# A decoder trunk on one core: retention's gate multiplied in two steps, and new constants in the planner's clock of transfers

## The chip, the core and the metric

The kernel runs on one core of a Trainium2 chip. The metric is the device time of one execution in microseconds (us); the median of three runs is given. A traced execution also gives a span, from the first to the last instruction, which is shorter than the device time.

## The reference

Two decoder layers on 256 rows of width 1024, all in float32. Cut to what matters:

```python
for i in range(DEPTH):                       # 2 layers
    h = rms_norm(x, norm_g[i])
    rq, rk, rv, rz, mq, mk, mv, mz = split(h @ w_in[i])          # eight groups of 512 columns
    r_out = retention(rotary(rq), rotary(rk), rv, ret_norm_g[i]) # 4 heads, GroupNorm per head
    r_out = silu(rz) * r_out                                     # retention's gate
    m_out = silu(mz) * moba(rms_norm(mq), rms_norm(mk), mv, rel_bias)
    x = x + concatenate([r_out, m_out]) @ w_out[i]
    gate = sigmoid(rms_norm(x) @ w_ple_gate[i])
    x = x + gate * rms_norm(p[i] @ w_ple[i], ple_norm_g[i])
```

silu(z) is computed as z * (tanh(z/2) + 1) / 2, with the half folded into a factor elsewhere.

## The kernel before

Every weight matmul is made of three TensorE rows: weights and activations are split into a high part (rounded to the matmul's reduced float32) and a low part (the rest), and `mm3` (L360 to L362) adds high x high, high x low and low x high in PSUM. A tile of weights, 128 x 1024, is loaded by SP into one of eight `wst` buffers (L316), its high part is made by a CAST on ScalarE (L321), its low part by a subtract on VectorE (L323), and twelve TensorE rows then use it. Activations reach the form that TensorE needs through `halves` (ScalarE copies a tile into 16-bit halves, L522), `turned` (SP issues a transposing DMA, L532, and VectorE copies the result out, two L541) and `to_parts` (a factor by L555 where there is one, the high part by ScalarE, L558, the low part by VectorE, L560). `a` is such a pair of parts, and m = 0, 1 are the two halves of 128 rows.

A layer runs the projections in the order MQ, MK, RQ, RK, MZ, MV, RV, RZ, with attention's and retention's own matmuls put between them, then the output projection (its second half of rows first, since MoBA's result is ready earlier), then the embedding `embed`, then the gate projection, whose result (`gated`: tanh L1031, two VectorE steps L1034 and L1036) becomes the next layer's `a`. Four PSUM banks `acc` serve the projections in turn, two to a group; a bank is free when its last reader is done.

The order on each engine is not written by hand. `Flow` plans it while the program is built: each piece of work outside TensorE is a generator that yields `ask(engine, cost, ...)`, and the planner lays it in an order given by its own clocks for the five engines and `dma`, a clock for the transfers. With these clocks it decides when SP issues a load and when it issues a transposing DMA (`can`, `backlog`, `lay`; `mb` is a load's size in MB, 0 marks a transposing DMA). All costs in it are constants in the text, and they set the order alone; what runs waits on semaphores.

Retention's end, before: after the matmuls L834, `ret_norm` computes statistics on VectorE, a power on GpSimd (L574) and the normed output RO on ScalarE (four L913 for each m). Apart from that, when RZ's projection is done, `gate` computes tanh on ScalarE (L755) and G = (tanh + 1) * projection on VectorE (L759), which frees the bank of RZ. `ret_gate` then multiplies RO by G (L932) and hands the product to `halves`, `turned` and `to_parts`, which make rows 0 to 3 of `yT`, read by the first half of the output projection.

Of the kernel before, what the change touches and what calls it, by code (L numbers as in the profile page):

```python
# [10 lines left out]
F32 = mybir.dt.float32  # L11
F32R = mybir.dt.float32r
U16 = mybir.dt.uint16
AF = mybir.ActivationFunctionType
ALU = mybir.AluOpType
AX = mybir.AxisListType

P = 128
# [7 lines left out]
GW = 512  # L26
# [55 lines left out]
class Flow:  # L82
# [4 lines left out]
    def __init__(self, slots):  # L87
        self.clock = {PE: 0.0, ACT: 3.0, DVE: 1.0, POOL: 1.0, SP: 0.7}
        self.dma = 0.0
        self.live = []  # L90
        self.free_at = {k: [0.0] * n for k, n in slots.items()}
        self.lent, self.lending = [], False
        self.loaded, self.after_turn = 0.0, False
        self.end = 0.0

    def begin(self, gen, key, at=None):
# [11 lines left out]
    def can(self, c):  # L108
        eng, cost, take, after, mb = c.want
        r = c.ready if c.on in (None, eng) else c.ready + HOP  # L110
        for w in after:
            if not w.done:
                return None
            r = max(r, w.ready + HOP)
        for s in take:
            if not self.free_at[s]:
                return None
            r = max(r, min(self.free_at[s]))
        if mb is None:
            return r  # L120
        r = max(r, self.dma - self.backlog())
        if mb and callable(c.key) and r < c.key():
            for o in self.live:
                if o.want[0] == SP and o.want[4] == TURN:
                    t = self.can(o)
                    if t is not None and t < r + AHEAD:
                        r = max(r, t + 1.3)
        return r

    def backlog(self):  # L130

        return 9.0 if self.dma < 14 else 1.6 if self.dma < 60 else 0.7

    def pick(self):
        by = {}
# [14 lines left out]
    def lay(self, start, c):  # L150
        eng, cost, take, after, mb = c.want
        for s in take:
            t = min(self.free_at[s])
            self.free_at[s].remove(t)
            self.got = None
            for i, (at, names) in enumerate(self.lent):
                if s == "w" and at == t:
                    self.got = self.lent.pop(i)[1]
                    break
        if eng == POOL and start - self.clock[POOL] > 1.5:  # L160
            cost += 0.9
        self.end = self.clock[eng] = start + cost
        c.ready, c.on = self.end, eng
        if mb is not None:
            rate = 3.3 if self.dma < 11 else 2.5
            if mb and self.after_turn:
                self.dma += 1.0
            self.after_turn = not mb
            self.dma = max(self.dma, start + (1.3 if mb else 1.0)) + (rate * mb if mb else 1.4)
            c.ready = self.dma + (0.9 if mb else 0.65)  # L170
            if mb:
                self.loaded = start
            else:
                c.ready += 0.75 * max(0.0, self.loaded + 2.6 - start)
        c.next()
        if c.done:
            self.live.remove(c)
# [57 lines left out]
def ask(eng, cost, take=(), after=(), mb=None):  # L235
    return eng, cost, take, after, mb
# [3 lines left out]
def tile_hybrid_trunk(ctx: ExitStack, tc: tile.TileContext, first, rest, x, pT, ple_g, rel_bias,  # L240
# [277 lines left out]
    def halves(src, name):  # L518

        yield ask(ACT, 0.95, take=("u16",))  # L520
        u = tok_p.tile([P, 2, GW], U16, name="u16", bufs=U_BUFS)
        nc.scalar.copy(u, src.bitcast(U16).rearrange("p (n t) -> p t n", t=2))  # L522
        if name:
            flow.free(name)
        return u
# [37 lines left out]
    def made(a, m, k0, c):  # L563
        for k in range(k0, k0 + 4):
            a.made[m, k] = c
        return c
# [110 lines left out]
    def layer(l, aT):  # L677
# [3 lines left out]
        def stats(m):  # L681
            return ST_X[l, m, "v"]

        def need_stats(m):
            return (ST_X[l, m],)
# [76 lines left out]

        def after_proj(g, m, ps):
            fn, slack = {MQ: (qk_norm, -3 if l else 2), MK: (qk_norm, -3 if l else 0), RQ: (rope, 4), RK: (rope, 2), MZ: (gate, 4),
                         MV: (value, 1), RV: (value, -4), RZ: (gate, -4)}[g]
            c = flow.begin(fn(g, m, ps), flow.soon(slack))
            {MV: VC, RV: VC, MZ: GC, RZ: GC}.get(g, TC)[g, m] = c
            if g == RZ:
                YC[m, 0] = made(yT, m, 0, flow.begin(ret_gate(m), flow.soon(-5)))

        def project(gs, by_m=False):
            ps = {}
# [151 lines left out]
            flow.lend("T", "T")  # L924
            flow.lend("V", "PS")

        def ret_gate(m):
            while m not in RC:
                yield ask(DVE, 0.0, after=(GC[RZ, m],))
            yield ask(DVE, 0.605, take=("tok",), after=(RC[m], GC[RZ, m]))  # L930
            y = tok_p.tile([P, GW], F32, name="tok")
            nc.vector.tensor_tensor(y, RO[m], G[RZ][:, m], op=ALU.mult)  # L932
            if m:
                flow.free("G")
                flow.free("T")
                flow.lend("T", "G")
            u = yield from halves(y, "tok")
            yield from to_parts(yT, m, 0, u, par[:, Q_RG + l * H:Q_RG + (l + 1) * H])

# [208 lines left out]
```

## Time and profile before

| | |
|---|---|
| median of 3 runs | 306.11 us (305.75 to 306.51) |
| the profiled execution | 305.53 us, span 303.6 us |
| granted TensorE clock | 0.998 |
| busy: TensorE, VectorE, ScalarE, GpSimd | 298.5, 249.8, 208.4, 31.9 us |
| instructions | 4209 |
| read from HBM | 57.42 MB |

The profiled execution lies 0.58 us below the median and 1.93 us above its own span. In rows of the trace the first number is the start in us from the span's start and the second the time in us that the row took; "x2" says that it stands for two instructions, and square brackets give the idle time of the engine before it and what ended it. TensorE rows overlap (a row of 512 columns is listed with 0.39 us), so their pace is read from their starts. SPq rows are the issue of a transfer by SP.

### The profile page before, as it was taken

The page shows a single profiled execution, that of the slowest core. Times are in us where ns is not written, and L with a number is a line of the kernel's source. Part 1 is how long each engine was busy: PE and PEld are TensorE (multiplying, and loading weights), DVE is VectorE, ACT ScalarE, POOL GpSimd, SP SyncE. Part 2 cuts the span into 40 slices and gives each one's busy share as a digit, 9 for nine tenths or more (in the row PEclk, how much of TensorE's full clock was granted, in tenths as well). Part 3 has the DMA queues.
Part 4 walks back from the last instruction along what each step waited for, and adds up shares of the span by engine and source line. Part 5 has one row for each costly group of instructions (what it writes and reads, how often), then busy time and mean ns, then how long its engine had stood idle before and what let it go on. Part 6 is the DMA issues. An engine that isn't in the chain of part 4 may idle for free.

```text
span 303.6 us, 4209 instructions
## 1 busy us (share of the span) xinstructions
PE 298.5 (98%) x1393; PEld 248.3 (82%) x1393; DVE 249.8 (82%) x459; ACT 208.4 (69%) x356; POOL 31.9 (11%) x44
## 2 busy tenths in 40 slices
PE   8999999999999999999999999999999999999994
PEld 4888888888888888888888888888888888888883
DVE  4996897996989897889988789986589689879932
ACT  4976949956746966978567894937473787598411
POOL 6005200000003000130001220000000040001100
PEclk9999999999999999999999999999999999999999
DMA  7998999989699295786697879577966964967011
GB/s 255 400 404 319 293 263 255 193 203 348 242 253 407 85 225 202 164 253 229 150 264 183 304 181 258 109 197 193 353 271 143 350 271 120 310 178 204 22 71 69
DMA packets 61773, 69.76 MB, mean 230 GB/s; under 512 B 46260, under 2 KB 47032, under 8 KB 61624
## 3 DMA queue, kind: packets, MB, share of 16 engines
q1 hardware_dynamic: 61712, 69.50, 75.6%
q8 instruction: 11, 0.18, 0.2%
q14 instruction: 10, 0.08, 0.1%
q0 software_dynamic: 32, 0.01, 0.0%
q10 hardware_dynamic: 8, 0.00, 0.0%
HBM read 57.42 MB, written 1.05 MB: 193 GB/s over the span
## 4 chain that ended last, share of the span: by engine, by line
PE 98%; DVE 0%; ACT 0%; issue 0%
PE acc L362 28%; PE acc L361 28%; PE acc L360 28%; PE acc L456 4%; PE mix L834 4%; PE mix L823 2%; PE mix L275 1%; PE mix L651 1%; PE mix L653 1%; PE mix L652 1%; PE mix L885 1%; PE mix L886 1%; ACT tmp L1031 0%; DVE tmp L1034 0%; DVE x_t L1036 0%
## 5 line engine op out<-in xcount | busy, mean ns | idle before, releaser
L360 PE MATMUL acc<-wh,a 128*128 128x512 f32 (+1 forms) x332 | 128.4, 387 | 0.0
L361 PE MATMUL acc<-wl,a 128*128 128x512 f32 (+1 forms) x332 | 127.5, 384 | 0.0
L362 PE MATMUL acc<-wh,a 128*128 128x512 f32 (+1 forms) x332 | 127.5, 384 | 0.0
L323 DVE TENSOR_TENSOR wl<-wst,wh 128x1024 fp32r<-128x1024 f32 x83 | 100.0, 1222 | 17.2 <-ACT wh L321 16.0
L321 ACT CAST wh<-wst 128x1024 fp32r<-128x1024 f32 x83 | 85.6, 1056 | 34.1 <-DMA wst<-in_w_in 23.7
L362 PEld LDWEIGHTS acc<-wh,a 128*128 128x128 f32 x332 | 62.4, 188 | 12.3
L360 PEld LDWEIGHTS acc<-wh,a 128*128 128x128 f32 x332 | 62.4, 188 | 12.2
L361 PEld LDWEIGHTS acc<-wl,a 128*128 128x128 f32 x332 | 62.4, 188 | 12.2
L522 ACT COPY u<-tok 128x1024 uint16<-128x1024 uint16 x30 | 30.9, 1049 | 8.0 <-DVE tok L852 3.8
L558 ACT CAST a<-tmp 128x512 fp32r<-128x512 f32 x20 | 12.3, 618 | 15.8 <-DVE tmp L541 7.4
L574 POOL TENSOR_TENSOR ro<-rs_t,neghalf 128x4 f32<-128x4 f32 x4 | 6.8, 1688 | 128.8 <-DVE rs_t L572 128.8
L541 DVE COPY tmp<-w 128x512 uint16<-128x512 uint16 x40 | 16.0, 451 | 1.8 <-DMA w<-u 1.8
L522 ACT COPY u<-x_t 128x1024 uint16<-128x1024 uint16 x12 | 12.5, 1045 | 5.0 <-DVE x_t L1036 3.8
L560 DVE TENSOR_TENSOR a<-tmp,a 128x512 fp32r<-128x512 f32 x20 | 13.6, 683 | 2.7 <-ACT a L558 2.7
L1031 ACT ACTIVATE tmp<-acc,hr 128x512 f32<-128x512 f32 (+1 forms) x9 | 5.7, 637 | 13.6 <-PE acc L362 9.3
L541 DVE COPY T<-w 128x512 uint16<-128x512 uint16 x32 | 12.4, 459 | 1.7 <-DMA w<-u 1.7
L715 POOL TENSOR_TENSOR qr<-qms,neghalf 128x4 f32<-128x4 f32 x8 | 9.9, 1314 | 28.8 <-DVE qms L713 28.7
L1034 DVE SCALAR_TENSOR_TENSOR tmp<-tmp,E 128x512 f32<-128x512 f32 (+1 forms) x9 | 5.6, 627 | 7.9 <-ACT tmp L1031 7.9
L834 PEld LDWEIGHTS mix<-V,PS 128*128 128x128 f32 x96 | 11.3, 192 | 0.3
L834 PE MATMUL mix<-V,PS 128*128 128x128 f32 x96 | 11.4, 275 | 0.0
L321 ACT CAST T<-wst 128x1024 fp32r<-128x1024 f32 x8 | 8.4, 1048 | 3.8 <-DMA wst<-in_w_ple 1.9
L574 POOL TENSOR_TENSOR r<-rs_t,neghalf 128x1 f32<-128x1 f32 x4 | 4.0, 992 | 54.8 <-DVE rs_t L572 54.8
(116 smaller groups left out, 367.1 us busy)
## 6 DMA issues: line engine op xcount, KB each, us to landing
wst<-in_w_in SPq DMA_DIRECT2D x60, 512.0 KB, 6.8
wst<-in_w_out SPq DMA_DIRECT2D x16, 512.0 KB, 8.8
wst<-in_w_gate SPq DMA_DIRECT2D x16, 512.0 KB, 4.9
wst<-in_w_ple SPq DMA_DIRECT2D x4, 512.0 KB, 7.5
wst<-in_rest SPq DMA_DIRECT2D x4, 384.0 KB, 6.8
a<-in_rest SPq DMA_DIRECT2D x3, 384.0 KB, 5.0
x_t<-in_x SPq DMA_DIRECT2D x1, 1024.0 KB, 10.4
gb<-in_ple_g SPq DMA_DIRECT2D x2, 512.0 KB, 10.2
```

The lines of the kernel that those rows point to most:

```text
L321: nc.scalar.copy(hi, s)
L323: nc.vector.tensor_tensor(lo, s, hi.bitcast(F32), op=ALU.subtract)
L360: nc.tensor.matmul(ps, ah, wh[:, cols], start=start, stop=False)
L361: nc.tensor.matmul(ps, ah, wl[:, cols], start=False, stop=False)
L362: nc.tensor.matmul(ps, al, wh[:, cols], start=False, stop=stop)
L456: nc.tensor.matmul(ps[m], (a0.lo if which[0] == "lo" else a0.hi)[:, k, m * P:(m + 1) * P], w, start=start and i == 0, stop=stop and i == 2)
L522: nc.scalar.copy(u, src.bitcast(U16).rearrange("p (n t) -> p t n", t=2))
L541: nc.vector.tensor_copy(v, w[:, t].rearrange("p (h b) k -> p h (b k)", h=v.shape[1]))
L558: nc.scalar.copy(h, src)
L560: nc.vector.tensor_tensor(a.lo[:, k0:k0 + 4, m * P:(m + 1) * P], src, h.bitcast(F32), op=ALU.subtract)
L574: nc.gpsimd.tensor_tensor(dst, t[:, :n], neghalf[:, :n], op=ALU.pow)
L834: nc.tensor.matmul(ps[:, h * DH:(h + 1) * DH], lhs(h, m, b), v[:, b, h * DH:(h + 1) * DH], start=b == 0, stop=b == m)
```

## The change

1. For RZ, `gate` is no longer used. A new `ret_tanh` computes tanh on ScalarE (L930); `ret_gate` first multiplies RO by RZ's projection, straight from PSUM (L940), and then computes (tanh + 1) * that product in place (L945). So RZ's bank is free only after L945, and no G is stored for RZ. MZ keeps `gate`.
2. The planner's clock of transfers has new constants and a new form: loads and transposing DMAs run from the time that SP issued them (`issued`), a load follows a transposing DMA with 1.2 us more and a transposing DMA costs 0.9 us of the clock, and the backlog to which it lets loads run ahead is 9.9, 2.5 and 1.6 us where it was 9.0, 1.6 and 0.7. This alters the order on all engines, in both layers. The number and kind of the instructions that compute or move data stays as it was.

```diff
--- before.py
+++ after.py
@@ -90,7 +90,7 @@
         self.live = []
         self.free_at = {k: [0.0] * n for k, n in slots.items()}
         self.lent, self.lending = [], False
-        self.loaded, self.after_turn = 0.0, False
+        self.issued, self.turning = 0.0, False
         self.end = 0.0
 
     def begin(self, gen, key, at=None):
@@ -118,6 +118,7 @@
             r = max(r, min(self.free_at[s]))
         if mb is None:
             return r
+        c.issue = r
         r = max(r, self.dma - self.backlog())
         if mb and callable(c.key) and r < c.key():
             for o in self.live:
@@ -129,7 +130,7 @@
 
     def backlog(self):
 
-        return 9.0 if self.dma < 14 else 1.6 if self.dma < 60 else 0.7
+        return 9.9 if self.dma < 14.9 else 2.5 if self.dma < 60.9 else 1.6
 
     def pick(self):
         by = {}
@@ -162,16 +163,15 @@
         self.end = self.clock[eng] = start + cost
         c.ready, c.on = self.end, eng
         if mb is not None:
-            rate = 3.3 if self.dma < 11 else 2.5
-            if mb and self.after_turn:
-                self.dma += 1.0
-            self.after_turn = not mb
-            self.dma = max(self.dma, start + (1.3 if mb else 1.0)) + (rate * mb if mb else 1.4)
-            c.ready = self.dma + (0.9 if mb else 0.65)
+            at = max(self.issued, c.issue) if self.dma > 14.9 else start
+            self.issued = at + cost
             if mb:
-                self.loaded = start
+                rate = 3.3 if self.dma < 11.9 else 2.55
+                self.dma = max(at + 2.27 + rate * mb, self.dma + rate * mb + 1.2 * self.turning)
             else:
-                c.ready += 0.75 * max(0.0, self.loaded + 2.6 - start)
+                self.dma = max(at + 3.05, self.dma + 0.9)
+            self.turning = not mb
+            c.ready = self.dma
         c.next()
         if c.done:
             self.live.remove(c)
@@ -762,11 +762,11 @@
 
         def after_proj(g, m, ps):
             fn, slack = {MQ: (qk_norm, -3 if l else 2), MK: (qk_norm, -3 if l else 0), RQ: (rope, 4), RK: (rope, 2), MZ: (gate, 4),
-                         MV: (value, 1), RV: (value, -4), RZ: (gate, -4)}[g]
+                         MV: (value, 1), RV: (value, -4), RZ: (ret_gate, -5)}[g]
             c = flow.begin(fn(g, m, ps), flow.soon(slack))
             {MV: VC, RV: VC, MZ: GC, RZ: GC}.get(g, TC)[g, m] = c
             if g == RZ:
-                YC[m, 0] = made(yT, m, 0, flow.begin(ret_gate(m), flow.soon(-5)))
+                YC[m, 0] = made(yT, m, 0, c)
 
         def project(gs, by_m=False):
             ps = {}
@@ -924,16 +924,27 @@
             flow.lend("T", "T")
             flow.lend("V", "PS")
 
-        def ret_gate(m):
+        def ret_tanh(m, ps, mark):
+            yield ask(ACT, 0.59, take=("tmp",), after=need_stats(m))
+            mark.tile = tmp_p.tile([P, GW], F32, name="tmp")
+            nc.scalar.activation(mark.tile, ps, AF.Tanh, scale=stats(m)[1])
+            flow.reach(mark)
+
+        def ret_gate(g, m, ps):
+            th = Mark()
+            flow.begin(ret_tanh(m, ps, th), flow.soon(-5))
             while m not in RC:
-                yield ask(DVE, 0.0, after=(GC[RZ, m],))
-            yield ask(DVE, 0.605, take=("tok",), after=(RC[m], GC[RZ, m]))
+                yield ask(DVE, 0.0)
+            yield ask(DVE, 0.605, take=("tok",), after=(RC[m],))
             y = tok_p.tile([P, GW], F32, name="tok")
-            nc.vector.tensor_tensor(y, RO[m], G[RZ][:, m], op=ALU.mult)
+            nc.vector.tensor_tensor(y, RO[m], ps, op=ALU.mult)
             if m:
-                flow.free("G")
                 flow.free("T")
                 flow.lend("T", "G")
+            yield ask(DVE, 0.605, after=(th,))
+            nc.vector.scalar_tensor_tensor(y, th.tile, 1.0, y, op0=ALU.add, op1=ALU.mult)
+            flow.free("acc")
+            flow.free("tmp")
             u = yield from halves(y, "tok")
             yield from to_parts(yT, m, 0, u, par[:, Q_RG + l * H:Q_RG + (l + 1) * H])
 
```

Where this moves instructions, three places follow: word for word the rows of each engine's order, "x2" for two instructions. Lines of the changed text behind the edit are 11 higher.

In the second layer, VectorE from retention's gate to the first L560 that makes rows 0 to 3 of `yT` (`tok` is the product, L323 are subtracts for weights that come later). Before:

```order
L759 SCALAR_TENSOR_TENSOR G<-tmp,acc 128x512
L932 TENSOR_TENSOR tok<-T,G 128x512
L323 TENSOR_TENSOR wl<-wst,wh 128x1024 x2
L759 SCALAR_TENSOR_TENSOR G<-tmp,acc 128x512
L932 TENSOR_TENSOR tok<-T,G 128x512
L323 TENSOR_TENSOR wl<-wst,wh 128x1024 x2
L541 COPY tmp<-w_2648 128x512 x2
L555 TENSOR_TENSOR tmp<-tmp,par 128x512
L323 TENSOR_TENSOR G<-wst,T 128x1024
L560 TENSOR_TENSOR a<-tmp,a 128x4x128
```

Now, with L940 and L945 for L759 and L932:

```order
L940 TENSOR_TENSOR tok<-T,acc 128x512
L945 SCALAR_TENSOR_TENSOR tok<-tmp,tok 128x512
L323 TENSOR_TENSOR wl<-wst,wh 128x1024
L940 TENSOR_TENSOR tok<-T,acc 128x512
L945 SCALAR_TENSOR_TENSOR tok<-tmp,tok 128x512
L323 TENSOR_TENSOR wl<-wst,wh 128x1024
L541 COPY tmp<-w_2658 128x512 x2
L555 TENSOR_TENSOR tmp<-tmp,par 128x512
L323 TENSOR_TENSOR G<-wst,T 128x1024
L323 TENSOR_TENSOR wl<-wst,wh 128x1024
L560 TENSOR_TENSOR a<-tmp,a 128x4x128
```

From the first product to the L560 there are four subtracts where there were five, and two of them stand behind the copies L541 where there was one.

Between the layers, VectorE from behind the sum of the first `gated` tile to the first L560 that makes the second layer's input (`x_t` is the residual; L1045 and L1047 are L1034 and L1036 of before). Before:

```order
L323 TENSOR_TENSOR wl<-wst,wh 128x1024
L323 TENSOR_TENSOR G<-wst,T 128x1024
L323 TENSOR_TENSOR wl<-wst,wh 128x1024 x2
L1034 SCALAR_TENSOR_TENSOR tmp<-tmp,E 128x512
L1036 TENSOR_TENSOR x_t<-x_t,tmp 128x512
L323 TENSOR_TENSOR T<-wst,T 128x1024
L541 COPY tmp<-w_1556 128x512 x2
L555 TENSOR_TENSOR tmp<-tmp,par 128x512
L1034 SCALAR_TENSOR_TENSOR tmp<-tmp,E 128x512
L1036 TENSOR_TENSOR x_t<-x_t,tmp 128x512
L323 TENSOR_TENSOR PS<-wst,V 128x1024
L560 TENSOR_TENSOR a<-tmp,a 128x4x128
```

Now:

```order
L323 TENSOR_TENSOR G<-wst,T 128x1024
L323 TENSOR_TENSOR wl<-wst,wh 128x1024 x3
L1045 SCALAR_TENSOR_TENSOR tmp<-tmp,E 128x512
L541 COPY tmp<-w_1561 128x512 x2
L555 TENSOR_TENSOR tmp<-tmp,par 128x512
L1047 TENSOR_TENSOR x_t<-x_t,tmp 128x512
L323 TENSOR_TENSOR T<-wst,T 128x1024
L560 TENSOR_TENSOR a<-tmp,a 128x4x128
```

One L1034, one L1036 and one subtract that stood between that sum and its L560 now stand behind the L560.

In the second layer, SP from the last transposing DMA of the attention's probabilities to those of MoBA's result (`pf` and `gb` are the embedding's input and gain). Before:

```order
L532 DMA_TRANSPOSE w_2138<-u_2123 128x8x128
L316 DMA wst<-in_w_in 128x1024 x3
L532 DMA_TRANSPOSE w_2202<-u_2191 128x8x128
L532 DMA_TRANSPOSE w_2213<-u_2200 128x8x128
L316 DMA wst<-in_w_in 128x1024 x7
L293 DMA pf<-in_pT 128x512
L316 DMA wst<-in_w_in 128x1024
L293 DMA gb<-in_ple_g 128x1024
L532 DMA_TRANSPOSE w_2398<-u_2385 128x8x128
L532 DMA_TRANSPOSE w_2420<-u_2414 128x8x128
L316 DMA wst<-in_w_in 128x1024
L316 DMA wst<-in_w_out 128x1024 x8
```

Now:

```order
L532 DMA_TRANSPOSE w_2149<-u_2134 128x8x128
L316 DMA wst<-in_w_in 128x1024 x3
L532 DMA_TRANSPOSE w_2223<-u_2215 128x8x128
L532 DMA_TRANSPOSE w_2235<-u_2221 128x8x128
L316 DMA wst<-in_w_in 128x1024
L293 DMA pf<-in_pT 128x512
L316 DMA wst<-in_w_in 128x1024
L293 DMA gb<-in_ple_g 128x1024
L316 DMA wst<-in_w_in 128x1024
L316 DMA wst<-in_w_out 128x1024 x7
L532 DMA_TRANSPOSE w_2419<-u_2405 128x8x128
L532 DMA_TRANSPOSE w_2442<-u_2433 128x8x128
```

Nine loads of `w_in` stood behind the pair of transposing DMAs in the middle, now three: six have moved ahead of this piece, and seven loads of the output weights now stand ahead of MoBA's pair, where one load of `w_in` and all eight stood behind it.

## The prediction

> **What bounds the kernel.** I read the page first, then who waits for whom on TensorE, then TensorE's rows in order of time, and last the rows of the other engines ahead of the places where TensorE is served latest.
>
> ```profile
> span 303.6 us, 4209 instructions
> PE 298.5 (98%) x1393; PEld 248.3 (82%) x1393; DVE 249.8 (82%) x459; ACT 208.4 (69%) x356; POOL 31.9 (11%) x44
> ...
> PE 98%; DVE 0%; ACT 0%; issue 0%
> ```
>
> TensorE is busy in 298.5 of 303.6 us, and the chain that ended last is TensorE in 98%. That busy time could still hide waits, since its rows overlap. The view of who waited has only this for TensorE:
>
> ```profile
> PE mix L275 <- PEq L1137: 0.8, 1, 0.8
> ```
>
> So I take the starts. First the normal pace, then the two places where the pace breaks, then the end:
>
> ```profile
> 217.15 0.40 PE L360 MATMUL acc<-wh,a 128*128 128x512 f32 x1
> 217.39 0.39 PE L361 MATMUL acc<-wl,a 128*128 128x512 f32 x1
> ...
> 220.79 0.39 PE L361 MATMUL acc<-wl,a 128*128 128x512 f32 x1
> ```
>
> ```profile
> 4.63 1.68 PE L456 MATMUL acc<-wh,a 128*128 128x512 f32 x4
> 6.15 0.62 PE L456 MATMUL acc<-wl,a 128*128 128x512 f32 x2
> ...
> 261.00 0.50 PE L362 MATMUL acc<-V,a 128*128 128x512 f32 x1
> 261.33 0.40 PE L360 MATMUL acc<-V,a 128*128 128x512 f32 x1
> ```
>
> ```profile
> 298.94 0.28 PE L362 MATMUL acc<-wh,a 128*128 128x256 f32 x1
> ```
>
> From 217.15 to 220.79 there are 16 steps, 0.2275 us each: a row of 512 columns starts as soon as the one before is streamed. Four rows take 1.52 us from 4.63 to 6.15, where 4 x 0.2275 = 0.91 were due: 0.61 lost while the first blocks arrive. At 261.00 a step takes 0.33: 0.10 lost. All other steps, taken through the whole trace, are at pace, to some 0.1 us in sum. So TensorE loses about 0.7 us to waits in the whole execution, and of the 4.7 us from the last matmul's start at 298.94 to the end at 303.6 the change alters nothing: the same tanh, two VectorE steps and transfer stand there in both orders.
>
> That is the main reading. The profiled execution took 305.53; 0.3% of the median (306.11) is 0.92 us, about what a measurement of this kernel can tell from no change. Removing every wait of TensorE would bring 0.7. The question is therefore whether the new order makes TensorE wait where it did not.
>
> **The change part by part.**
>
> *The operations themselves.* For RZ in two layers and two halves, four L759 and four L932 become four L940 and four L945; tanh stays.
>
> ```profile
> L759 DVE SCALAR_TENSOR_TENSOR G<-tmp,acc 128x512 f32<-128x512 f32 x8 | 5.4, 688 | 2.3 <-ACT tmp L755 2.3
> L932 DVE TENSOR_TENSOR tok<-T,G 128x512 f32<-128x512 f32 x4 | 2.8, 692 | 0.1
> ```
>
> L759 reads PSUM (`acc`) and takes 688 ns, L932 reads SBUF alone and takes 692: where an operand lies makes no difference here, so the new pair costs 1.38 us, as the old one. Cost 0 on VectorE. What can be gained is latency: L940 needs no tanh.
>
> *Retention's gate in the second layer, the place with the 0.10.* The matmul at 261.00 reads the low part that L560 makes.
>
> ```profile
> 250.65 0.69 DVE L932 TENSOR_TENSOR tok<-T,G 128x512 f32<-128x512 f32 x1
> 251.26 2.36 DVE L323 TENSOR_TENSOR wl<-wst,wh 128x1024 fp32r<-128x1024 f32 x2
> 253.53 0.68 DVE L759 SCALAR_TENSOR_TENSOR G<-tmp,acc 128x512 f32<-128x512 f32 x1
> ...
> 257.13 0.79 DVE L541 COPY tmp<-w 128x512 uint16<-128x512 uint16 x2
> ...
> 260.26 0.68 DVE L560 TENSOR_TENSOR a<-tmp,a 128x512 fp32r<-128x512 f32 x1
> ```
>
> ```profile
> 249.20 0.70 ACT L755 ACTIVATE tmp<-acc,hr 128x512 f32<-128x512 f32 x1
> 249.77 2.02 ACT L321 CAST wh<-wst 128x1024 fp32r<-128x1024 f32 x2
> ```
>
> ```profile
> 252.75 1.24 SPq L532 DMA_TRANSPOSE w<-u  x1
> ```
>
> ```profile
> DMA to landing us min/median/max: 3.0/3.1/4.8
> ```
>
> The last row is for all 42 transposing DMAs. Before, the product was ready at 250.65 + 0.69 = 251.34 and L560 ended at 260.94, 9.60 later, with five subtracts of 1.18 between (2.36 for two). Now one cast (2.02 / 2 = 1.01) stands ahead of tanh on ScalarE that stood behind it; the tanh may start up to 1.01 later, and the product, which then needs one VectorE step behind tanh and not two, is ready 0.69 sooner behind it: between 0.69 earlier and 0.3 later. I take 251.3, between these ends; at 251.6 the cover below is 0.2 and not 0.5. With one subtract less, VectorE would reach the end of L560 at 260.94 - 1.18 = 259.8. The other limit is the transposing DMA: if SP issues it at 252.75 as before, it lands at 252.75 + 3.1 = 255.85, and L541, L555 (as long as L932), now two subtracts, and L560 follow: 0.79 + 0.69 + 2.36 + 0.68 = 4.52, to 260.4. TensorE wants it by 260.9 (261.00 less the 0.10). I take 260.4: the wait of 0.10 goes, cover 0.5. With the longest landing, 4.8, it is 262.1 and the wait 1.2 in place of 0.10: a loss of 1.1. What speaks for a long landing is that SP now issues four gate loads ahead of this DMA; against it, those need a free buffer each and will be issued as the subtracts before 251 release them, some in time to be through.
>
> At this place a page speaks against the change. The Trainium skill, "DMA: Bandwidth & Descriptors", section "Two DMAs through the same engine are not ordered", says that descriptors within one queue of one engine start in order. By that rule a transposing DMA behind loads pays for them, and the sum would be the 1.1 us loss just given, or more with several loads; by the median row it is 0.10 gained. The trace agrees as far as 4.8 against 3.0, no further.
>
> *The bank.* RZ's second bank was freed by L759 at 253.53 + 0.68 = 254.21. It is next written, by the second half of the output projection, here:
>
> ```profile
> 255.79 0.39 PE L360 MATMUL acc<-wh,a 128*128 128x512 f32 x1
> ```
>
> Cover 1.58. Now L945 frees it: 251.34, a subtract, L940, L945, so 251.34 + 1.18 + 0.69 + 0.69 = 253.9. Behind it wait this bank's matmul and with it all of TensorE. Cost 0, cover 1.9; in the first layer the same order stands with more room.
>
> *Between the layers.* VectorE makes the second layer's first input:
>
> ```profile
> 140.01 0.69 DVE L1036 TENSOR_TENSOR x_t<-x_t,tmp 128x512 f32<-128x512 f32 x1
> ...
> 151.53 0.69 DVE L560 TENSOR_TENSOR a<-tmp,a 128x512 fp32r<-128x512 f32 x1
> ```
>
> ```profile
> 152.36 0.41 PE L362 MATMUL acc<-T,a 128*128 128x512 f32 x1
> ```
>
> L560 ends at 152.22, 0.14 before the matmul that reads it. An L1034 (of the form of L759, so 0.69), an L1036 and a subtract now stand behind it: 0.69 + 0.69 + 1.18 = 2.56 us sooner, if the transposing DMA is there. TensorE did not wait, so the gain is 0; the cover grows to about 2.7, and even a landing 1.7 late leaves 1.0.
>
> *Weights of MV and RV in the second layer.*
>
> ```profile
> 190.44 10.19 SPq L532 DMA_TRANSPOSE w<-u  x5
> 200.68 1.53 SPq L316 DMA_DIRECT2D wst<-in_w_in  x3
> 207.15 2.62 SPq L532 DMA_TRANSPOSE w<-u  x2
> 209.82 4.24 SPq L316 DMA_DIRECT2D wst<-in_w_in  x7
> ```
>
> ```profile
> 205.12 1.05 ACT L321 CAST wh<-wst 128x1024 fp32r<-128x1024 f32 x1 [4.80 <-DMA wst<-in_w_in]
> ```
>
> ```profile
> 215.93 1.23 DVE L323 TENSOR_TENSOR wl<-wst,wh 128x1024 fp32r<-128x1024 f32 x1 [1.98 <-ACT wh L321]
> ```
>
> SP's loads wait for the queue's turn behind the transposing DMAs, ScalarE then idles 4.80 for a load, and a subtract ends at 217.16, only 0.23 before L361 at 217.39 reads it. Six loads have moved ahead of this stretch. They gain at least one place each, 4.24 / 7 = 0.6 us, and at most the 10.19 us of the five transposing DMAs, unless no buffer is free, when they gain nothing. I take the low end, 0.6: cover 0.8, time 0. The loads moved ahead also push transposing DMAs, by up to 1.7 (4.8 less 3.1) each; MoBA's pair, which now stands behind seven loads, is wanted only when the output projection starts, after all of RZ: 0.
>
> *Sum.* 303.6 - 0.10 + 0 = 303.5 of span, 305.4 of device time for an execution like the profiled one, which lies 0.58 under the median: 306.0.
>
> **The rivals.**
>
> *Transposing DMAs come late behind the loads* (slower). Place and price as above: behind the four gate loads, TensorE waits from a landing of 3.6 on (cover 0.5), it counts as slower from 4.6, and at 4.8 it costs 1.1: 306.11 + 1.1 = 307.2. For it: 4.8 occurs. Against: the median is 3.1.
>
> *TensorE waits for RZ's bank* (slower). It decides once L945 ends after 255.79. For it: the bank now hangs on the normed output too, which passes GpSimd and ScalarE. Against: a cover of 1.9. A slip of 3 costs 1.1: 307.2.
>
> *A low part comes late at one of the many other moved subtracts* (slower): covers of 0.14 and 0.23 show how near the old order ran to waiting; one subtract out of place costs up to 1.18: 307.3.
>
> *The waits go* (faster): all 0.7 would give 305.4. Against: 0.61 of it stands at the start, where the first loads are ordered as before.
>
> *TensorE waits so long that it slows down.* The trace shows a slow pace only at the start:
>
> ```profile
> 0.76 4.00 PE mix L275 x9
> ```
>
> Nine rows of 512 columns take 0.44 us each, nearly twice 0.2275, for 4.0 us, which is 1.95 lost. A wait of 3 us followed by as long a stretch at that pace would cost 5: 311. No wait in this trace is over 0.61.
>
> The Trainium skill, "TensorE: Matmul & The Clock Gate", section "What's actually happening", has TensorE's clock halved after an idle window of about 3.4 us; no wait in this trace is long enough to show it, and that figure is the page's.
>
> **How the numbers follow.** No measurable change: 0.81, 306.0, its own range 305.5 to 306.6 from the spread of the three runs. Late transposing DMAs 0.06, bank 0.03, another late part 0.05, long wait 0.01: slower by over 0.3%, 0.15 in all. Faster by over 0.3%: 0.04, the 0.7 plus the spread. The range goes from 305.2 to 307.4, over the three slower cases at 307.2 and 307.3.
>
> **What would show it.** Right: TensorE's steps stay 0.2275 at 261, 152 and 217, tanh (L930) no longer ahead of both products, L560 earlier than 260.9 by about 0.5. Wrong: a step longer than 0.3 behind the gate loads, at the output projection's second half or at a weight's first use; or a larger gain, if the end of the program got shorter, which I do not see.

## The result, and the profile after

The change made the kernel slower: 307.92 us median of 7 runs (307.13 to 309.46) against 306.04 of before (305.36 to 306.51). The means stand at a ratio of 1.0071, with a 95% interval of 1.0046 to 1.0095; the loss is under 2% and clear of the noise. The profiled execution took 308.94, the second longest of the seven, so it shows about 1 us more of waiting than a middle one. Its totals:

```profile
span 306.7 us, 4243 instructions
PE 299.5 (98%) x1393; PEld 247.6 (81%) x1393; DVE 249.5 (81%) x459; ACT 206.7 (67%) x356; POOL 30.7 (10%) x44
...
PE 49%; DVE 20%; DMA 15%; ACT 7%; issue 6%; SPq 1%; DVEq 0%; ACTq 0%
```

Each engine works about as long as before. What changed is the chain: TensorE held 98% of it, now 49%, and half of it passes through VectorE, the DMAs and ScalarE. The view of who waited has three names for TensorE, besides the first blocks' loads, that were not there:

```profile
PE acc L362 <- DVE a L560: 1.0, 1, 1.0
PE acc L360 <- DVE tok L718: 0.5, 1, 0.5
PE mix L834 <- ACT V L749: 0.5, 1, 0.5
```

TensorE's rows in order of time show where they stand (the time in brackets is the idle time and what ended it):

```profile
27.38 0.39 PE L362 MATMUL acc<-wh,a 128*128 128x512 f32 x1
28.25 0.50 PE L360 MATMUL acc<-wh,a 128*128 128x512 f32 x1 [0.48 <-DVE tok L718]
```

```profile
92.60 0.39 PE L362 MATMUL acc<-wh,a 128*128 128x512 f32 x1
93.46 0.38 PE L834 MATMUL mix<-V,PS 128*128 128x128 f32 x1 [0.47 <-ACT V L749]
```

```profile
159.80 0.40 PE L361 MATMUL acc<-wl,a 128*128 128x512 f32 x1
161.15 0.50 PE L362 MATMUL acc<-wh,a 128*128 128x512 f32 x1 [0.95 <-DVE a L560]
```

Taken as steps against the pace of 0.2275, with the rows just behind that come in a little slow, these three cost 0.76, 1.14 (0.63 and 0.10 here, 0.31 and 0.10 at the next V) and 1.23; a fourth at 140.4 costs 0.26 (its matmul at 140.82 follows an L560 that ends at 140.77). Together they cost 3.39. Before lost none of it. Against that the start lost 0.12 less, the 0.10 at 261 is gone, and the end behind the last matmul's start was 0.25 shorter: 2.9 of the 3.1 by which the span grew, the rest being rows a few ns off pace.

All four waits lie in layer 1 or between the layers. Behind all of them stands a late VectorE, and behind all but the one at 27.4 it had idled at its copy L541 until a transposing DMA landed. The view of one line, L541, has for before and after:

```profile
  DMA w<-u: 4.3, 4
```

```profile
  DMA w<-u: 17.1, 16
```

VectorE idles 17.1 us there in place of 4.3. The largest piece is at 122, ahead of the wait at 159.8. SP's rows and VectorE's:

```profile
117.89 3.16 SPq L316 DMA_DIRECT2D wst<-in_w_in  x3
122.41 8.79 SPq L532 DMA_TRANSPOSE w<-u  x3
```

```profile
120.62 1.45 DVE L998 TENSOR_TENSOR x_t<-acc,x_t 128x512 f32<-128x512 f32 x2
127.49 0.79 DVE L541 COPY tmp<-w 128x512 uint16<-128x512 uint16 x2 [5.42 <-DMA w<-u]
```

Three loads stand right ahead of the transposing DMA of 122.41; it lands at 127.47, 5.06 after its issue, and VectorE, whose next step in order is the copy of its result, does nothing for 5.42. Before, the same DMA was issued at 119.82 with no load under way and landed after 3.09, and VectorE idled 0.59 at the copy:

```profile
119.82 2.96 SPq L532 DMA_TRANSPOSE w<-u  x2
```

In a table of one stretch, 122 to 136 us, whose columns are TensorE, its weight loads, VectorE, ScalarE and GpSimd, first before and then after:

```profile
122.00:136.00 14.00, 14.00 (x63) 11.62 (x62) 11.71 (x30) 11.76 (x24) 3.66 (x4) 1.00 0.78 199
```

```profile
122.00:136.00 14.00, 14.00 (x64) 11.58 (x63) 7.63 (x17) 10.59 (x20) 1.48 (x1) 1.00 0.74 173
```

VectorE does 7.63 us of work where it did 11.71. TensorE stands 1.9 us further on in the old trace at that time; in the stretch that matches, 120.1 to 134.1, VectorE did 10.20. A further transposing DMA, issued at 129.96, lands 4.86 later and costs VectorE another 0.91. It has nothing to spare afterwards (28.66 of the 29 us from 136 to 165), so the lateness reaches the L560 of 160.41 that TensorE then waits for. At 92.6 it goes another way round:

```profile
88.50 0.46 DVE L541 COPY tmp<-w 128x512 uint16<-128x512 uint16 x1 [1.53 <-DMA w<-u]
```

```profile
90.38 0.62 ACT L558 CAST a<-tmp 128x512 fp32r<-128x512 f32 x1 [4.26 <-DVE tmp L541]
...
92.20 0.62 ACT L558 CAST a<-tmp 128x512 fp32r<-128x512 f32 x1 [0.24 <-DVE tmp L541]
92.72 0.68 ACT L749 ACTIVATE V<-acc,rstd 128x512 f32<-128x512 f32 x1
```

This is MoBA's transposing pair of layer 1. Its first DMA is issued at 84.25 behind four loads of the output weights, two of them still under way, and lands 4.22 later:

```profile
72.64 4.63 SPq L316 DMA_DIRECT2D wst<-in_w_out  x4
84.25 3.13 SPq L532 DMA_TRANSPOSE w<-u  x2
```

TensorE does not need its result yet. But VectorE's copies wait for it, ScalarE's casts L558 wait for VectorE, and the V that TensorE does need stands behind the second cast on ScalarE. Before, the pair was issued at 81.61, ahead of these loads, its first DMA landed after 3.04, and V waited for TensorE:

```profile
87.32 0.62 ACT L558 CAST a<-tmp 128x512 fp32r<-128x512 f32 x1 [3.21 <-DVE tmp L541]
88.95 0.69 ACT L749 ACTIVATE V<-acc,rstd 128x512 f32<-128x512 f32 x1 [1.01 <-PE acc L362]
```

So the DMA lands 3.82 later than before, and only 1.18 of that is a longer landing. The other 2.64 is a later issue: the product L852 that it carries starts at 82.02 where it started at 79.38. One subtract and L674, which stood behind the product before, now stand ahead of it, and VectorE's subtracts on the way wait 2.67 us for weights, where they waited 2.46.

The wait at 27.4 is of a third kind. VectorE idles 0.91 ahead of a subtract whose load landed late, and the L718 that frees TensorE's bank stands behind that subtract. SP issued that load at 13.15, behind the load of a table (`tb`) that stood behind it before, when it went out at 11.62; ScalarE's cast of it starts at 25.28 in place of 22.62. VectorE's rows:

```profile
26.37 1.23 DVE L323 TENSOR_TENSOR wl<-wst,wh 128x1024 fp32r<-128x1024 f32 x1 [0.91 <-ACT wh L321]
27.51 0.68 DVE L718 TENSOR_TENSOR tok<-acc,qr 128x512 f32<-128x512 f32 x1
```

### The profile page after: what moved, and what is told of

Read it like the earlier page. It is cut to its first block, busy times and chain, and to the rows that moved or that the text cites. A ratio compares the mean times of both kernels' runs of the same rounds, so it can differ in the third digit from the quotient of the medians.

```text
span 306.7 us, 4243 instructions
## 1 busy us (share of the span) xinstructions
PE 299.5 (98%) x1393; PEld 247.6 (81%) x1393; DVE 249.5 (81%) x459; ACT 206.7 (67%) x356; POOL 30.7 (10%) x44
## 3 DMA queue, kind: packets, MB, share of 16 engines
HBM read 57.42 MB, written 1.05 MB: 191 GB/s over the span
## 4 chain that ended last, share of the span: by engine, by line
PE 49%; DVE 20%; DMA 15%; ACT 7%; issue 6%; SPq 1%; DVEq 0%; ACTq 0%
PE acc L362 15%; PE acc L360 15%; PE acc L361 15%; DMA w<-u 7%; DMA wst<-in_w_in 6%; DVE wl L323 5%; ACT wh L321 2%; DVE tmp L541 2%; DMA a<-in_rest 2%; PE mix L834 2%; DVE a L560 1%; ACT u L522 1%; DVE tmp L1045 1%; DVE E L641 1%; ACT T L913 1%
## 5 line engine op out<-in xcount | busy, mean ns | idle before, releaser
L360 PE MATMUL acc<-wh,a 128*128 128x512 f32 (+1 forms) x326 | 126.6, 388 | 0.5 <-DVE tok L718 0.5
L362 PE MATMUL acc<-wh,a 128*128 128x512 f32 (+1 forms) x326 | 125.7, 386 | 1.0 <-DVE a L560 1.0
L361 PE MATMUL acc<-wl,a 128*128 128x512 f32 (+1 forms) x326 | 125.6, 385 | 0.0
L323 DVE TENSOR_TENSOR wl<-wst,wh 128x1024 fp32r<-128x1024 f32 x82 | 99.0, 1219 | 11.9 <-ACT wh L321 11.5
L321 ACT CAST wh<-wst 128x1024 fp32r<-128x1024 f32 x82 | 84.4, 1052 | 18.5 <-DMA wst<-in_w_in 12.3
L362 PEld LDWEIGHTS acc<-wh,a 128*128 128x128 f32 x326 | 61.2, 188 | 13.8 <-DVE a L560 1.4
L360 PEld LDWEIGHTS acc<-wh,a 128*128 128x128 f32 x326 | 61.3, 188 | 13.1 <-DVE tok L718 0.9
L361 PEld LDWEIGHTS acc<-wl,a 128*128 128x128 f32 x326 | 61.3, 188 | 11.9
L522 ACT COPY u<-tok 128x1024 uint16<-128x1024 uint16 x30 | 30.9, 1046 | 17.1 <-DVE tok L740 7.4
L541 DVE COPY tmp<-w 128x512 uint16<-128x512 uint16 x40 | 16.4, 455 | 13.6 <-DMA w<-u 13.6
L558 ACT CAST a<-tmp 128x512 fp32r<-128x512 f32 x20 | 12.4, 621 | 21.1 <-DVE tmp L541 12.4
L574 POOL TENSOR_TENSOR ro<-rs_t,neghalf 128x4 f32<-128x4 f32 x4 | 7.6, 1912 | 129.1 <-DVE rs_t L572 129.1
L522 ACT COPY u<-x_t 128x1024 uint16<-128x1024 uint16 x12 | 12.5, 1043 | 8.8 <-DVE x_t L998 6.1
L541 DVE COPY T<-w 128x512 uint16<-128x512 uint16 x32 | 12.6, 456 | 2.5 <-DMA w<-u 2.4
L560 DVE TENSOR_TENSOR a<-tmp,a 128x512 fp32r<-128x512 f32 x20 | 13.6, 682 | 0.0
L1045 DVE SCALAR_TENSOR_TENSOR tmp<-tmp,E 128x512 f32<-128x512 f32 (+1 forms) x9 | 5.6, 628 | 8.2 <-ACT tmp L1042 8.2
L362 PE MATMUL acc<-T,a 128*128 128x512 f32 (+1 forms) x30 | 11.4, 379 | 0.0
L360 PE MATMUL acc<-T,a 128*128 128x512 f32 (+1 forms) x30 | 11.3, 375 | 0.0
```

The costliest lines, as they stand in the source:

```text
L321: nc.scalar.copy(hi, s)
L323: nc.vector.tensor_tensor(lo, s, hi.bitcast(F32), op=ALU.subtract)
L360: nc.tensor.matmul(ps, ah, wh[:, cols], start=start, stop=False)
L361: nc.tensor.matmul(ps, ah, wl[:, cols], start=False, stop=False)
L362: nc.tensor.matmul(ps, al, wh[:, cols], start=False, stop=stop)
L541: nc.vector.tensor_copy(v, w[:, t].rearrange("p (h b) k -> p h (b k)", h=v.shape[1]))
```

## The experiments

Ratios are to the kernel before on the same chip, with 95% intervals. "Late" counts the transposing DMAs in a trace that landed more than 3.5 us after their issue (of 36 to 40 whose landing was recorded): 6 before, 14 after. "Idle" is VectorE's idle time in us ahead of its copies of their results: 4.3 before, 17.1 after. Both are counted in one traced execution of each kernel, which lies up to 1.35 us off that kernel's median. The letters stand for theories; each is stated in the expectation that first uses it.

**Which half of the change.** First the gate alone, with the old clock of transfers.

> The gate's new steps with the order's old clock of transfers. Theory A (the refitted clock lets loads go so early that transposing DMAs land behind them, and VectorE runs late): no part of the loss without it, 305.4 to 306.5 us, ratio to before 0.998 to 1.002, transposing DMAs that land after more than 3.5 us about 6, as before (after: 14). Theory B (splitting the gate moves steps and banks so that TensorE waits): the whole loss, 307.5 to 308.5, ratio about 1.006. Theory C (any other order costs about as much, since the old constants were chosen for the old order): 306.8 to 308, with waits at other places than after's 27.4, 92.6 and 159.8.

e1 took 305.79, ratio 0.9987 (0.9970 to 1.0005), with 9 late and an idle time of 3.8. There is no loss. The only new wait of TensorE in its trace is 0.61 for a subtract at 217.5, where the prediction had read a cover of 0.23. Theory B falls. Then the clock alone, with the gate's code as before.

> The order's new clock of transfers with the gate as it was. Theory A: the whole loss, 307.5 to 308.5 us, ratio 1.005 to 1.009, and over ten transposing DMAs that land after more than 3.5 us. Theory B: none of it, 305.7 to 306.4. Theory C: 306.8 to 308, the same as with the gate alone.

e2 took 307.26, ratio 1.0037 (1.0015 to 1.0058), with 11 late, an idle time of 11.5, and the wait at the same V as above:

```profile
PE mix L834 <- ACT V L749: 1.3, 1, 1.3
```

The loss comes with the clock. It is smaller than expected, though its interval overlaps that of the whole change. Whether the other half needs both parts or is a matter of which order came out, these two runs can't tell.

**The lead of the loads.** The changed kernel with the old lead, and the old kernel with the new:

```
-        return 9.9 if self.dma < 14.9 else 2.5 if self.dma < 60.9 else 1.6
+        return 9.0 if self.dma < 14 else 1.6 if self.dma < 60 else 0.7
```

> The changed kernel with the old lead of loads (9.0, 1.6, 0.7 and the old two limits in place of 9.9, 2.5, 1.6): a load is ordered 0.9 us nearer to its turn. If it is the loads ahead of transposing DMAs that cost (A), fewer land late and most of the loss goes: 306.0 to 307.0 us, ratio 1.000 to 1.003, late ones under ten. If the lead doesn't matter (B, C): 307.5 to 308.5.

> The kernel before with only the new lead (9.9, 2.5, 1.6 with the new limits): in the old clock, which counts a load's delivery apart, this lets each load be ordered 0.9 us further ahead. A: more transposing DMAs land behind loads, over ten late ones, 306.8 to 308 us, ratio 1.002 to 1.006. B: nothing, 305.7 to 306.4.

e3: 307.35, ratio 1.0039 (1.0019 to 1.0059); late 7, idle 11.8. Fewer land late, as theory A said, but half of the loss stays. The traced execution of e3 took 306.45, the shortest of twelve, and its trace shows TensorE waiting only 0.41 behind the first blocks, at a V; it can't show where the middle one loses. e4: 305.46, ratio 0.9992 (0.9974 to 1.0009), and here theory A breaks:

```profile
DMA to landing us min/median/max: 3.0/3.4/6.2
```

15 transposing DMAs are late, one by more than any in the changed kernel, and nothing is lost: VectorE idles 6.3. This suggests that a late transposing DMA costs only where the order puts its copy at the head of VectorE's line too early. The old clock added up to 1.64 us to its landing behind a fresh load (0.75 x (2.6 - 0.42), since a load holds SP's clock for 0.42), so that other work could stand ahead of the copy.

**Four edits of the clock.** In the changed kernel the old surcharge put back (e5, `c.ready += 0.75 * max(0.0, self.loaded + 2.6 - at)` behind a load); in the old kernel the same line taken out (e6); in the changed kernel `AHEAD = 4.0` for 1.6 (e7), and `at = start` for the line that dates a DMA's issue (e8).

> The changed kernel, whose clock again adds to the landing of a transposing DMA what the old one did behind a load (0.75 us for each us by which the load stands less than 2.6 ahead). Theory D (the new clock forecasts transposing DMAs behind loads 0.5 us too early in the mean, VectorE's order is made for that forecast, and VectorE then idles): the idle time of VectorE before L541 falls from 17.1 us to under 8, and most of the loss goes, 305.8 to 306.8 us, ratio 0.999 to 1.003. Theory C (any other order costs, chance decides): 306.8 to 308. Theory E (it is the loads' issue and landing times in the new clock that are wrong, not the transposing DMAs): no change from 307.9 beyond 0.5.

> The kernel before, whose clock no longer adds anything to a transposing DMA's landing behind a load; nothing else changed. Theory D: part of the loss appears, 306.5 to 307.5 us, ratio 1.002 to 1.005, VectorE's idle time before L541 8 to 14 us in place of 4.4. Theory E: no change, 305.7 to 306.4, idle under 7. Theory C: 306.8 to 308.

> The changed kernel with AHEAD at 4.0 in place of 1.6: a load that is not urgent is ordered behind a transposing DMA that is to be issued within 4.0 us. If loads right ahead of the transposing DMAs are the cause, whatever the forecast, late ones fall from 14 to under 8 and the time to 306.0 to 307.0; by D also, since the forecast is then true. By C 306.8 to 308. It may cost at weights that come later: then waits of TensorE on L323 or L321 show, and up to 309.

> The changed kernel with its new clock, but a DMA's issue is again taken where the order puts it, not where it could stand if SP never held it. Theory E: most of the loss goes, 306.0 to 306.8. Theory D: it stays, 307.2 to 308.3, VectorE idle before L541 over 11 us. C: 306.8 to 308.

e5: 306.51, 1.0022 (1.0009 to 1.0035). Two thirds of the loss are gone, as D expected, but the idle time is 12.5 and not under 8. e6: 306.42, 1.0021 (1.0005 to 1.0037); the time came out near what D expected, but the idle time, 6.0, did not, and the one long wait, 0.8 at 219.7, is for a subtract at a weight's first use and not for anything behind a copy. e7: 306.12, 1.0010 (0.9995 to 1.0025): holding loads back behind a coming transposing DMA removes nearly all of the loss, though 11 are still late. e8: 310.94, 1.0158 (1.0129 to 1.0186), outside what any theory gave. Loads now come too late for the weights:

```profile
PE acc L361 <- DVE wl L323: 3.3, 4, 1.5
```

In e8 the waits at 92.6 and 159.8 are gone and VectorE idles only 5.0 at its copies, yet the late weights cost more than the whole change did. So e8 does not decide on theory E: without the new dating of issues one loss goes and a larger one comes. It does show that idle time alone is no measure of the loss: it counts only where somebody on TensorE's path stands behind it.

**The price of a transposing DMA alone.** e9 is the changed kernel with the old price (queue 1.4, landing 0.25 later, surcharge); e10 the old kernel with the new price, `self.dma = max(start + 2.15, self.dma + 0.9)` and no surcharge; e12 is e10's edit on e4; e11 is e4's lead with the new gate.

> The changed kernel and its new clock, in which a transposing DMA alone is again priced as before: it keeps the queue for 1.4 in place of 0.9, lands 0.25 later behind others, and later still behind a fresh load. Theory D (the loss comes from forecasting transposing DMAs too early): the loss goes, 305.6 to 306.7 us, ratio 0.999 to 1.002. Theory F (it is the pace of the loads, 1.28 us for each half megabyte where the old clock held them to 1.85): it stays, 307.3 to 308.3. Theory C (chance): anything from 306 to 308.

> The kernel before with one thing of the new clock: a transposing DMA keeps the queue for 0.9 and lands with its turn, with nothing added behind a load. Loads are priced as before. D: most of the loss appears, 306.8 to 308 us, ratio 1.003 to 1.007, VectorE idle before L541 over 8 us (4.3 before). F: no change, 305.7 to 306.4.

> The new gate with the old clock and the longer lead, the two that did not lose alone (0.9987 and 0.9992). If they add, 305.0 to 305.7 us, ratio 0.996 to 0.999; by theory C (each order has its own waits) 305.4 to 307.

> The old clock with the longer lead, under which 15 transposing DMAs landed late (up to 6.2 us) at no loss, and now with the new price of a transposing DMA. D: as many are late and the order does not expect it, so the loss is as large as after's or larger, 307.3 to 309 us, VectorE idle before L541 over 12 us (6.3 without). F: 305.4 to 306.4, since the loads are priced as in the run without loss.

e9: 307.57, 1.0052 (1.0034 to 1.0070). e10: 305.65, 0.9992 (0.9980 to 1.0004), with an idle time of 9.5. Both speak against theory D as I had put it: the price alone neither makes the loss in the old order nor takes it from the new one. In e9's trace the waits at 92.6 and 159.8 are gone, but VectorE still idles 4.72 at the copy of the place at 122, is busy for 14.68 of the next 15.10 us, and TensorE waits at 140.4 (lines are 4 higher in this kernel):

```profile
PE acc L366 <- DVE her L641: 1.1, 1, 1.1
```

e11: 305.99, 1.0004 (0.9990 to 1.0017); the two that lost nothing alone do not add to a gain, and no version here beats the kernel before by a measurable amount. e12: 311.60, 1.0180 (1.0162 to 1.0199), late 17, idle 18.2 (lines are 1 lower in this kernel):

```profile
PE acc L360 <- DVE wl L322: 1.4, 2, 1.2
PE mix L833 <- ACT V L748: 1.2, 1, 1.2
```

That is more than theory D had expected. Both paths, by VectorE's subtracts and by ScalarE's V, are in its trace. VectorE idles 2.52 at a copy at 54.9 and is then busy without a break until the subtract for which TensorE waits 1.19 at 62.3; it idles 3.63 at a copy at 91.1, ScalarE's cast 6.37 behind it, and V is late again. With the lead of e4 the new price costs 6 us; without it, nothing. In the old clock both must come together: loads close enough ahead to delay the transposing DMAs, and an order made as if they did not. Theory F is not needed for a loss, since e12's loads are priced as e4's; but e9 came out where F said, so the new pace of the loads may still be a second cause. Theory C in its plain form, that any other order costs, falls with e1, e4, e7, e10 and e11, five other orders at no measurable loss.

**The same order with half the bytes.** Every run so far changed the order itself. The last four keep each engine's order and take bytes off the queue. In e13 34.62 MB are read where 57.42 were, and the casts and subtracts, which then read one half twice, take as long as before (1.04 and 1.20 us on average):

```
-            nc.sync.dma_start(s, self.src[:, 2 * c:2 * c + 2])
+            n = 1 if len(cut) in range(9, 999) else 2
+            cut.append(0)
+            nc.sync.dma_start(s[:, :n], self.src[:, 2 * c:2 * c + n])
+            if n == 1:
+                s = s[:, :1].to_broadcast([P, 2, GW])
```

> The changed kernel with every engine's order as it is, but each weight load from the tenth on brings only half of its bytes (the first of two blocks, which cast and subtract then read twice): part of the weights is left out. Theory G (the order is sound, its transfers come later than it was made for): with the queue relieved nearly all waits go, except the one at 27.4, whose load is not halved: 305.6 to 306.6 us, and within 0.8 of the order before with the same halved loads. Theory H (steps stand in a wrong sequence on the engines, whatever the transfers do): 307 to 308, over 1.0 above it.

> The control: the order before with its weight loads halved in the same way from the eleventh on (part of the weights is left out). TensorE hardly waited for transfers there, so by every theory 305.2 to 306.2 us, ratio 0.997 to 1.001.

> The changed kernel's order with only the 14 loads issued between 98 and 137 us halved (part of the weights is left out). If the stall of 1.2 at 159.8 comes from the transposing DMA at 122.4 that lands 5.06 later behind three loads, and the one at 130.0 behind it: it lands within 3.6, VectorE's idle time there falls by over 3 us, the stall shrinks to under 0.3, time 306.4 to 307.2. If the stall comes from the sequence of steps on VectorE: it stays, 307.5 to 308.3.

> The changed kernel's order with only the 20 loads issued between 38 and 77 us halved (part of the weights is left out). If ScalarE's V comes late at 92.6 because the transposing DMA at 84.25 lands 4.2 later behind loads: it lands within 3.3, the waits of TensorE at 92.6 and 94.6 (0.63 and 0.31) go, time 306.6 to 307.4. If it comes from the sequence on ScalarE: they stay, 307.5 to 308.3.

The new order with halved loads: 306.06, 1.0014 (1.0004 to 1.0025); late 4. The old one: 305.58, 0.9995 (0.9984 to 1.0006). Four fifths of the loss go with the bytes, and of what stays against the control, 0.0019, the trace shows one wait behind the first blocks, for the bank of 27.4 (lines are 6 higher in these kernels), whose load stands ahead of the halved ones:

```profile
PE acc L366 <- DVE tok L724: 0.2, 1, 0.2
```

Theory G holds, H falls: the order would be sound if its transfers came when it was made to expect them. Which transfers, the loads or the transposing DMAs, e13 does not tell, since it makes both come earlier.

Halving only the 14 loads around 98 to 137 us gives 306.95, 1.0036 (1.0022 to 1.0050). SP's and VectorE's rows at the place of 122:

```profile
117.69 3.16 SPq L320 DMA_DIRECT2D wst<-in_w_in  x3
122.20 6.76 SPq L538 DMA_TRANSPOSE w<-u  x3
```

```profile
125.26 0.80 DVE L547 COPY tmp<-w 128x512 uint16<-128x512 uint16 x2 [3.04 <-DMA w<-u]
```

The same three loads stand ahead, the DMA lands 3.04 after its issue in place of 5.06, VectorE idles 3.04 in place of 5.42 (I had expected over 3 less; it is 2.38), and TensorE's wait for the L560 is gone. The DMA was issued only 0.21 sooner, so here it is the landing that counts. The transposing DMA behind it, issued at 127.73, still lands after 4.86, against my expectation. TensorE's wait at 92.9 stays, as it should, since nothing ahead of it was halved:

```profile
PE mix L840 <- ACT V L755: 0.3, 1, 0.3
```

Halving only the 20 loads of 38 to 77 us gives 306.72, 1.0034 (1.0022 to 1.0047). MoBA's first transposing DMA is issued at 81.94, where it was 84.25, and lands 3.08 later, where it was 4.22; VectorE no longer waits at its copy, and V is made in time:

```profile
87.02 0.62 ACT L564 CAST a<-tmp 128x512 fp32r<-128x512 f32 x1 [2.65 <-DVE tmp L547]
...
89.80 0.69 ACT L755 ACTIVATE V<-acc,rstd 128x512 f32<-128x512 f32 x1 [0.27 <-PE acc L368]
```

V now waits for TensorE, not TensorE for V. Of the 3.45 us by which the DMA lands sooner, 2.31 are an earlier issue, since VectorE gets its weights sooner and so reaches the product that the DMA carries sooner (79.71 for 82.02), and 1.14 are a shorter landing. TensorE's first wait there was 0.63, so by these rows either might have been enough (an estimate); e16 does not part them. The wait at 27.4 stays (0.6), and that at 159.8 shrinks to 0.2, though no load near it was halved. The DMA of the place at 122 is issued 1.52 sooner there and lands after 4.29 in place of 5.06, so that VectorE's copy starts 2.29 sooner and TensorE's matmul only 1.38; why it lands sooner behind the same three loads was not tried. Each of the two runs gives back about half of the loss, e15 at the place where the bytes were taken off, e16 there and at 159.8.

## Why the prediction was wrong

The prediction was 306.0 us, with a range of 305.2 to 307.4; the kernel took 307.92.

*Right, by its own steps.* What bounds the kernel was right, and so was that no gain was to be had. The pair of operations costs nothing (L940 and L945 take 686 and 692 ns). Retention's gate in the second layer came out as worked out there:

```profile
256.55 0.69 DVE L945 SCALAR_TENSOR_TENSOR tok<-tmp,tok 128x512 f32<-128x512 f32 x1
...
262.33 0.68 DVE L560 TENSOR_TENSOR a<-tmp,a 128x512 fp32r<-128x512 f32 x1
```

TensorE runs 3.43 us behind the old trace here. Less that, the second bank is free at 253.81 (predicted 253.9), and L560 ends at 259.58 (predicted 260.4), so that the wait of 0.10 is gone and its matmul at 264.43 finds it 1.41 early (predicted 0.5). The size is partly luck: on that scale the transposing DMA behind the gate loads was issued at 251.81 where 252.75 was taken, and it landed after 3.35 where 3.1 was taken; 4.8 was feared. The weights of RV have 6.93 us to spare where 0.8 was taken as the low end. The gate alone (e1) lost nothing.

*Wrong: the cost of transposing DMAs pushed by loads, taken as 0.* The prediction saw that loads move ahead of transposing DMAs and push them by up to 1.7 each, and then closed with "MoBA's pair, which now stands behind seven loads, is wanted only when the output projection starts, after all of RZ: 0". In layer 2 that was so: the pair cost TensorE nothing. In layer 1, where four of these loads now stand ahead of MoBA's pair, TensorE lost 1.14, and by a path which that sentence leaves out. It asked who reads the result, and not who stands behind the instruction that waits for it: VectorE's next steps behind L541, and ScalarE's V behind L558. e16 shows that this loss goes when the loads of that stretch bring half of their bytes; it does not show how much of it is the landing (1.14 us shorter) and how much the earlier issue (2.31 us). At 122 it is the landing: e15 took 2.02 off it, and the wait of 1.23 was gone.

*Wrong: the first rival's place and size.* "Transposing DMAs come late behind the loads" was the mechanism, with 0.06 and 1.1 us, at one place in the second layer. It struck at 84 and 122 us, in layer 1 and between the layers, and it added up: 2.4 us there in the profiled execution, 0.26 more at 140.4, and 0.76 by a late load at 27.4. The places shown and priced were the second layer's and the one between the layers; "the many other moved subtracts" went into one rival of 0.05. The cover said to grow between the layers, to 2.7 and 1.0 at worst, was the first L560's; it had 0.84 left, and the next L560 was the late one. A sum over the places in layer 1 was not made.

*The loads ahead.* The prediction weighed the Trainium skill, "DMA: Bandwidth & Descriptors", section "Two DMAs through the same engine are not ordered", by which descriptors of one queue start in order on an engine. That rule names no time; that loads ahead delay a transposing DMA is what I drew from it, and the traces bear this out. Over six of them (before, after, e1 to e4) the landing of a transposing DMA by the number of loads still under way at its issue is: none 3.06 us median (88 of them), one 3.23 (94), two 3.69 (33), three 4.66 (8). e15 agrees: half the bytes ahead, 3.04 for 5.06. I took the median row over all 42 and should have taken the row by loads ahead, which the trace of before already had: 3.06 with none (17), 3.20 with one (17), 3.82 with two (3).

*The pace.* The rival of a slow clock did not occur: the longest wait is 1.1, and steps behind it are at 0.2275 after one or two rows.

*What stays open.* It is not known which terms of the new clock make the order too early. e10 and e12 show that in the old clock the price of a transposing DMA does it only together with loads that run close ahead, and e9 that the old price does not cure the new clock. What else is at fault there no run isolates; the pace of the loads and the dating of their issue are not excluded. Nor is it explained why e2 lost about half of what the whole change lost, if it did. The wait at 27.4 was not tried by itself.

## What to carry to other kernels

A transfer that is late costs through the in-order queues behind the instruction that waits for it, so for each moved transfer list what stands behind its reader on that engine, and behind the next engine's waiting step, and not only who uses the result. Look also at when it is issued: at 84 us more of the lateness came from the issue than from the landing. When a scheduler's constants change, walk through every stage for the covers, the first layer like the last; a change that moves steps everywhere is not priced at the three places where the diff is easiest to read. To tell a bad sequence from late data, keep the order and take bytes off the queue: four such runs settled here what the edits of the planner had left open.

## What the runs showed of the hardware

The landing of a transposing DMA grows with the loads under way at its issue, by the four medians above. Five of the 88 that were issued with no load under way still landed late, after up to 4.90. The page has a queue that may bear on them:

```profile
q8 instruction: 11, 0.18, 0.2%
```

In the same six traces none of the 77 transposing DMAs that had neither a load under way nor a packet of this queue in flight landed late (3.43 at most), and five of the 11 that had such a packet did. Over all eighteen traces it is 5 of 270 against 25 of 41. The DMA at 129.96 is one of the five (packet from 132.81 to 133.78). At the same place before, it took 4.76, with one load and such a packet; with halved loads 3.07 in e13 and 3.04 in e14, but 4.86 in e15, each time with such a packet in flight. So a packet alone does not decide it, and since no run moves one by itself, it is not shown to be the cause.
